# Local attention, first query tile: score products that move 128 columns instead of 256

## The chip, the cores and the metric

The kernel runs on one core of one Trainium2 chip. The metric is the device time of one execution in microseconds; the time before is the median of three runs, 640.8 us (640.77 to 642.25). The profile is one further execution, recorded instruction by instruction. Engines are named as the profile names them: PE (matrix products), PEld (the loading of a product's stationary operand, which overlaps PE), DVE (vector), ACT (activations), POOL, and SP, which issues DMAs.

## The reference

One transformer block on 512 tokens of width 1024, all in float32. A first half of the heads does a block-sparse attention with three branches; the second half does local attention ("swa") with a window of 128 tokens, and this is the part concerned here:

```python
def swa_attention(q, k, v, sinks, slopes):      # 8 heads, 2 key groups, 64 wide
    ...
    dist = C + i - j                             # C = 128
    valid = (dist >= 0) & (dist < SWA_WINDOW) & (kpos >= 0)
    s = jnp.einsum('bnqgrd,bnkgd->bngrqk', qb, kb).astype(jnp.float32) * scale
    s = s - slopes_g[:, :, None, None] * dist.astype(jnp.float32)
    s = jnp.where(valid[:, None, None], s, NEG_INF)
    m = jnp.maximum(jnp.max(s, axis=-1, keepdims=True), sg)
    e = jnp.exp(s - m)
    prob = e / (jnp.sum(e, axis=-1, keepdims=True) + jnp.exp(sg - m))
    o = jnp.einsum('bngrqk,bnkgd->bnqgrd', prob.astype(vb.dtype), vb)
```

Each tile of 128 queries sees its own 128 keys and the 128 before them. The first tile of queries has no keys before it, so its scores fill 128 columns and not 256. After attention come an output projection, a gated feed-forward part with a short convolution, and a gated per-layer embedding.

## The kernel before

Matrix products are made in a split form: each operand is a rounded high part and the rest as a low part, both of type float32r, so that a product is a sum of two or three float32r products. A query tile already holds its high and low parts stacked over the 128 partitions, so a score needs two: `score` (line 954) multiplies the same stationary query block with the high part of the keys (`kh`) and then with the low part (`kl`), into the same place in PSUM. Plain float32 products occur too, for short sums and for transposes: `rstd_col` (line 571) multiplies four blocks of a [128, 512] tile with a column of ones, one matmul call for each (lines 575 and 576); `compress_out` (line 858) makes one call for the keys (line 870) and two for the values (lines 871 and 872); `transpose_split` (line 892) transposes through PE with a 128x128 identity.

The attention runs in units: for the sparse half and then for the local half, for two key groups `g` each, the query tiles in the order 3, 0, 2, 1 (lines 1137 and 1138). A local unit is `swa_scores` (line 958). For `qt == 0` it sets `n = 128`, starts at key 0, and reads the second half of the table of distances (`b0 = P`). For each of four heads it makes the two products of `score` into half of a PSUM tile (two heads to a tile, three tiles of the tag "s" in rotation), and a fused DVE instruction that adds the scaled distances and takes the row's minimum with the sink (lines 971 to 979). Then ACT makes four exponentials with row sums, DVE takes reciprocals, and POOL scales the four rows. In the unit after, `pv` (line 922) transposes these probabilities on PE, ACT and DVE split the transposed tile into its two parts, and PE multiplies it with the values.

Between these steps `fill` (line 537) puts in work from other parts, which needs only PE and weights: the remaining query projections and the first part of the output projection (`out_proj_first`, line 1200). The functions lay out what is to be done with priorities and dependencies; the order of the instructions on the engines in the attention part is then made by the planner of the surrounding framework, which goes through the program with its own timing model (line 55). From `ple_load`, a little after the attention, to the end of the feed-forward part, the order is written out by the kernel itself and kept.

All eight units of the local half call `swa_scores`; those with `qt == 0` are the second of each key group. The line numbers in the profile are those of two helpers: L419 stands for everything in the attention part, so instructions are told apart there by the names of their tiles (`swa_pss` is the PSUM tile of the local scores).

Of the kernel before, what the change touches and what calls it, by code (L numbers as in the profile page):

```python
# [15 lines left out]
ALU = mybir.AluOpType  # L16
# [406 lines left out]
class Block:  # L423
# [534 lines left out]
    def swa_scores(self, u):  # L958
        self.phase = "swa"
        nc = self.nc  # L960
        g, qt = u["g"], u["qt"]
        kh, kl = self.ks
        n = P if qt == 0 else 2 * P
        k0 = 0 if qt == 0 else (qt - 1) * P
        b0 = P if qt == 0 else 0

        p = self.u([P, 4, 2 * P + 1], F32, "p")
        ns = self.nsink[:, 4 * g : 4 * g + 4]
        nc.gpsimd.tensor_copy(p[:, :, n], ns)
        nm = self.tiny([P, 4], "nm")  # L970
        for r in range(4):
            if r % 2 == 0:
                ps = self.ps("s")
            o = ps[:, r % 2 * 256 : r % 2 * 256 + 256]
            self.score(ps, o, self.q[4 + 2 * g + r // 2][:, r % 2, qt * P : (qt + 1) * P],
                       kh[:, g, k0 : k0 + 256], kl[:, g, k0 : k0 + 256])
            nc.vector.tensor_tensor_reduce(p[:, r, :n], o[:, :n], self.dist_w[:, b0:], op0=ALU.add, op1=ALU.min,
                                           scale=SLOPES[4 * g + r], scalar=ns[:, r : r + 1], accum_out=nm[:, r : r + 1])
            yield 100 if r < 3 else 4 * n + 380
        sm = self.tiny([P, 4], "sm")  # L980
        for r in range(4):
            nc.scalar.activation(p[:, r, : n + 1], p[:, r, : n + 1], AF.Exp, bias=nm[:, r : r + 1], scale=-1.0,
                                 accum_out=sm[:, r : r + 1])
        rc = self.tiny([P, 4], "rc")
        nc.vector.reciprocal(rc, sm)
        for r in range(4):
            self.scale_rows(p[:, r, :n], rc[:, r : r + 1])
        yield 400
        u["blocks"] = [
            ([p[:, r, b * P : (b + 1) * P] for r in range(4)], P,  # L990
             self.vs[k0 // P + b][:, 4 + g].rearrange("p a d -> p (a d)"))
            for b in range(n // P)
        ]
# [1128 lines left out]
```

## Time and profile before

| | |
|---|---|
| median of three runs | 640.8 us (640.77 to 642.25) |
| the profiled execution, its own time | 641.23 us |
| its span, from the first instruction to the last | 639.5 us |
| the local attention's scores, first to last | 153.9 to 195.9 us from the span's start |
| score products on PE (`swa_pss`) | 64, each of 256 columns |

The profile page gives busy times by engine, the span in 40 slices, the chain of work that ended last, and the costliest groups. The time of an answer is counted from the span's start. Two readings need care. A matmul's recorded duration is its latency through the array, and matmuls are pipelined: what one costs PE in a row of others is the spacing of their ends, not the recorded duration. And for the timeline, instructions of one kind that follow each other are merged into one row with the stretch from the first start to the last end and their number.

### The profile page before, as it was taken

The numbers are of one execution on the slowest core, as the hardware profiler recorded it, in microseconds if no ns is written. First come the engines' busy times: TensorE is split into PE (matmuls) and PEld (weight loads), VectorE is DVE, ScalarE is ACT, GpSimd is POOL, SyncE is SP. The second block draws the span as 40 slices with busy tenths as digits, with TensorE's granted clock in tenths as the row PEclk, the third lists the DMA queues.
The fourth block names the chain that finished last, engine by engine and source line by source line (L and its number), as shares of the span: only waits on it lengthen the run. The fifth ranks groups of instructions, "written<-read, shape, count | busy, mean of one in ns | idle before, by whom it ended". The sixth has DMA issues, their size and how long they took to land.

```text
span 639.5 us, 11315 instructions
## 1 busy us (share of the span) xinstructions
PE 633.3 (99%) x4071; PEld 575.6 (90%) x4071; DVE 511.1 (80%) x1029; ACT 396.3 (62%) x759; POOL 155.1 (24%) x240
## 2 busy tenths in 40 slices
PE   8999999999999999999999999999999999999997
PEld 7988888888888887888999999999998899999986
DVE  6796668978866498799898989989898985756973
ACT  7545579878898567474677777777754533343251
POOL 1001497787686100211001010102000010201000
PEclk9999999999999999999999999999999999999999
DMA  8416834221321658485465766687754534377032
GB/s 303 176 60 181 226 84 126 51 49 36 75 59 63 228 224 324 149 210 120 123 191 145 202 164 153 169 213 238 178 156 121 152 92 122 114 250 264 1 116 81
DMA packets 45288, 95.78 MB, mean 150 GB/s; under 512 B 4400, under 2 KB 13744, under 8 KB 44976
## 3 DMA queue, kind: packets, MB, share of 16 engines
q1 hardware_dynamic: 40208, 84.49, 40.8%
q0 software_dynamic: 4880, 10.49, 9.7%
q8 instruction: 32, 0.52, 0.3%
q14 instruction: 24, 0.20, 0.1%
q10 hardware_dynamic: 144, 0.08, 0.0%
HBM read 81.41 MB, written 9.44 MB: 142 GB/s over the span
## 4 chain that ended last, share of the span: by engine, by line
PE 97%; ACT 1%; DMA 1%; DVE 0%; issue 0%; SPq 0%; ACTq 0%
PE mlpup_psmm L201 23%; PE fill_psmm L419 10%; PE mlpup_pss L201 8%; PE mlpdown_pst L201 6%; PE mlpdown_pss L201 5%; PE mlpup_pst L201 5%; PE mlpdown_psmm L201 4%; PE nsa_pss L419 3%; PE nsa_pst L419 3%; PE nsa_pso L419 3%; PE norm_pss L201 3%; PE projq_psmm L419 3%; PE mlpup_pso L201 2%; PE vnatural_pss L419 2%; PE projk_psmm L419 2%; PE compress_psmm L419 2%
## 5 line engine op out<-in xcount | busy, mean ns | idle before, releaser
L201 PE MATMUL mlpup_psmm<-r_u,mlpup_wh 128*128 128x256 f32 (+1 forms) x612 | 79.4, 283 | 0.1
L201 PEld LDWEIGHTS mlpup_psmm<-r_u,mlpup_wh 128*128 128x128 f32 x612 | 76.0, 191 | 0.6 <-DVE mlpup_wh L201 0.4
L201 PE MATMUL mlpup_psmm<-mlpup_u,mlpup_wh 128*128 128x256 f32 (+1 forms) x474 | 69.6, 298 | 0.0
L201 PEld LDWEIGHTS mlpup_psmm<-mlpup_u,mlpup_wh 128*128 128x128 f32 x474 | 63.5, 190 | 2.6
L201 POOL DMA_DIRECT2D mlpup_u<-in_gs_dram x17 | 20.9, 1230 | 154.9 <-DVE mlpup_s L201 61.0
L201 ACT ACTIVATE mlpup_wh<-mlpup_u 128x1024 fp32r<-128x1024 f32 x37 | 39.2, 1060 | 25.2 <-PE mlpup_psmm L201 21.2
L201 ACT ACTIVATE mlpdown_wh<-mlpdown_wr 128x1024 fp32r<-128x1024 f32 (+1 forms) x24 | 23.7, 988 | 40.1 <-PE mlpdown_pst L201 10.7
L201 DVE TENSOR_TENSOR mlpup_wh<-mlpup_u,mlpup_wh 128x1024 fp32r<-128x1024 f32 x37 | 45.2, 1221 | 1.4 <-ACT mlpup_wh L201 0.5
L419 PE MATMUL fill_psmm<-loadx_u,fill_wh 128*128 128x512 f32 x144 | 45.2, 398 | 0.0
L201 PE MATMUL mlpdown_pst<-mlpup_u,mlpdown_wh 128*128 128x512 f32 (+1 forms) x228 | 45.0, 340 | 0.0
L201 PEld LDWEIGHTS mlpdown_pst<-mlpup_u,mlpdown_wh 128*128 128x128 f32 x228 | 37.0, 189 | 5.0
L201 DVE TENSOR_TENSOR mlpdown_wh<-mlpdown_wr,mlpdown_wh 128x1024 fp32r<-128x1024 f32 (+1 forms) x24 | 27.3, 1138 | 16.6 <-ACT mlpdown_wh L201 16.3
L419 POOL TENSOR_SCALAR nsa_u<-nsa_u,nsa_nrc,gate 128x512 f32<-128x512 f32 (+3 forms) x64 | 38.5, 619 | 5.4 <-DVE nsa_nrc L419 3.2
L419 ACT ACTIVATE nsa_u<-nsa_u,nsa_nnm 128x512 f32<-128x512 f32 (+3 forms) x64 | 35.2, 553 | 4.0 <-DVE nsa_nnm L419 3.7
L201 DVE TENSOR_TENSOR mlpup_wh<-mlpup_wr,mlpup_wh 128x1024 fp32r<-128x1024 f32 (+1 forms) x23 | 27.9, 1211 | 11.9 <-ACT mlpup_wh L201 11.9
L201 PE MATMUL mlpdown_pss<-mlpup_u,mlpdown_wh 128*128 128x256 f32 x246 | 35.9, 282 | 0.0
L201 POOL TENSOR_TENSOR mlpdown_s<-mlpdown_s,mlpdown_s 128x512 f32<-128x512 f32 x6 | 9.6, 1599 | 105.0 <-ACT mlpdown_s L201 104.8
L419 DVE TENSOR_TENSOR nsa_u<-nsa_pst,nsa_u 128x512 fp32r<-128x512 f32 (+1 forms) x43 | 28.9, 687 | 7.5 <-ACT nsa_u L419 7.2
L201 PEld LDWEIGHTS mlpdown_pss<-mlpup_u,mlpdown_wh 128*128 128x128 f32 x246 | 32.5, 191 | 0.3
L419 ACT ACTIVATE nsa_u<-nsa_pst 128x512 fp32r<-128x512 f32 x43 | 25.0, 596 | 12.0 <-PE nsa_pst L419 11.4
L419 DVE CUSTOM_DVE_ANT_0 nsa_u<-nsa_pss,biastables_u 128x128 f32<-128x128 f32 (+4 forms) x64 | 27.7, 449 | 4.8 <-PE nsa_pss L419 2.7
L201 PE MATMUL mlpdown_psmm<-mlpup_u,mlpdown_wh 128*128 128x256 f32 (+1 forms) x180 | 31.1, 320 | 0.0
(341 smaller groups left out, 1653.0 us busy)
## 6 DMA issues: line engine op xcount, KB each, us to landing
mlpup_u<-in_gs_dram SPq DMA_DIRECT2D x34, 512.0 KB, 5.5
mlpup_u<-in_gs_dram POOLq DMA_DIRECT2D x17, 512.0 KB, 7.0
mlpup_wr<-in_gs_dram SPq DMA_DIRECT2D x17, 256.0 KB, 4.1
fill_wr<-in_win_dram SPq DMA_DIRECT2D x6, 512.0 KB, 4.3
fill_u<-fill_u SPq DMA_DIRECT2D x20, 128.0 KB, 2.3
mlpdown_wr<-in_down_dram SPq DMA_DIRECT2D x5, 512.0 KB, 3.8
loadx_u<-in_xT_dram SPq DMA_DIRECT2D x8, 256.0 KB, 5.0
compress_u<-projk_u SPq DMA_DIRECT2D x16, 128.0 KB, 4.0
```

What stands on the lines that cost most here:

```text
L201: return f(*map(real, a), **{m: real(x) for m, x in k.items()})
L419: hold(x.call(*map(real, x.a), **{m: real(v) for m, v in x.k.items()}))
```

## The change

In the local units the two products of `score` get the `n` columns that are read, and not always 256. The offset of a head's scores in its PSUM tile stays (0 or 256). For `qt` of 1 to 3, `n` is 256 and nothing differs; for `qt == 0` the 16 products (two groups, four heads, two parts) move 128 columns of keys each. The columns dropped are keys 128 to 255, whose scores were written to PSUM and not read. The DVE instruction reads the same 128 columns as before.

```diff
             if r % 2 == 0:
                 ps = self.ps("s")
-            o = ps[:, r % 2 * 256 : r % 2 * 256 + 256]
+            o = ps[:, r % 2 * 256 : r % 2 * 256 + n]
             self.score(ps, o, self.q[4 + 2 * g + r // 2][:, r % 2, qt * P : (qt + 1) * P],
-                       kh[:, g, k0 : k0 + 256], kl[:, g, k0 : k0 + 256])
-            nc.vector.tensor_tensor_reduce(p[:, r, :n], o[:, :n], self.dist_w[:, b0:], op0=ALU.add, op1=ALU.min,
+                       kh[:, g, k0 : k0 + n], kl[:, g, k0 : k0 + n])
+            nc.vector.tensor_tensor_reduce(p[:, r, :n], o, self.dist_w[:, b0:], op0=ALU.add, op1=ALU.min,
                                            scale=SLOPES[4 * g + r], scalar=ns[:, r : r + 1], accum_out=nm[:, r : r + 1])
             yield 100 if r < 3 else 4 * n + 380
```

## The prediction

> **What bounds the kernel now.** I read the page first: the engines' busy shares, the granted clock and the chain of work that ended last.
>
> ```profile
> span 639.5 us, 11315 instructions
> PE 633.3 (99%) x4071; PEld 575.6 (90%) x4071; DVE 511.1 (80%) x1029; ACT 396.3 (62%) x759; POOL 155.1 (24%) x240
> PEclk9999999999999999999999999999999999999999
> PE 97%; ACT 1%; DMA 1%; DVE 0%; issue 0%; SPq 0%; ACTq 0%
> ```
>
> PE is busy for 633.3 of 639.5 us, at the full granted clock in every slice, and the chain that sets the end lies on PE for 97% of the span. So a nanosecond taken from PE in a stretch where the chain is on PE is a nanosecond of the end, and one added is one added. Next I looked at the stretch of the change, which holds the local scores, and at the stretch behind it up to the part whose order is fixed. The columns are the stretch, its length, and the busy time (with the number of instructions) of PE, PEld, DVE, ACT and POOL; then the granted clock.
>
> ```profile
> 150.00:200.00 50.00, 49.86 (x298) 42.85 (x297) 38.74 (x142) 45.71 (x131) 40.96 (x74) 1.00 0.24 65
> 200.00:240.00 40.00, 40.00 (x189) 33.10 (x188) 27.68 (x41) 25.55 (x42) 6.15 (x8) 1.00 0.54 193
> ```
>
> PE idles 0.14 us in 50, and not at all in the 40 after. Better order cannot bring more than those 0.14 us here; the rest of any gain must be shorter PE work. ACT is the second engine, 45.71 of 50 us.
>
> The third view is the tile of the local scores: its forms, and what waits for it. The last two rows are the view's "who waited for it".
>
> ```profile
> L419 PEld LDWEIGHTS swa_pss<-projq_u,fill_u x64: 187/188/192, 153.9 to 195.7; 128*128 128x128 f32 x64
> L419 PE MATMUL swa_pss<-projq_u,fill_u x64: 274/282/365, 154.1 to 195.9; 128*128 128x256 f32 x64
> L419 DVE CUSTOM_DVE_ANT_0 swa_u<-swa_pss,biastables_u,nsink x32: 320/476/484, 160.8 to 197.3; 128x256 f32<-128x256 f32 x24, 128x128 f32<-128x128 f32 x8
> ...
> who waited for it (us, times):
>   DVE swa_u L419: 2.1, 5
> ```
>
> All 64 products move 256 columns; 8 of the 32 DVE instructions that read them read 128, and these are the two units of the first query tile. Their 16 products are the ones that change.
>
> **The change part by part.** No instruction is added, removed or given a new wait; no DMA is touched. 16 products become half as wide; the DVE instruction reads the same 128 columns. The whole sum is 16 times the difference in the spacing of a product on PE. The chain of work has the first four of them as PE time, and the timeline shows rows of the same kind in an unbroken run, beside wider ones:
>
> ```profile
> 161.59 0.48 PE swa_pss L419 x4
> ...
> 190.98 0.64 PE L419 MATMUL swa_pss<-projq_u,fill_u 128*128 128x256 f32 x4
> ...
> 177.45 2.48 PE L419 MATMUL fill_psmm<-nsa_u,fill_wh 128*128 128x512 f32 x10
> ...
> L419 PE MATMUL fill_psmm<-nsa_u,fill_wh 128*128 128x512 f32 x10 | 2.5, 393 | 0.0
> ```
>
> In the chain four products take 0.48 us, 0.120 each. In the timeline, four take 0.64 from the first start to the last end; less one latency of 0.282 that is 0.36 for three, again 0.119. Ten of 512 columns take 2.48, less 0.393 that is 2.09 for nine, 0.232 each. So 256 more columns cost 0.113, or 0.44 ns a column, and 128 columns at that rate would take 0.120 - 0.056 = 0.064 us.
>
> But a product also loads its stationary operand, here 128x128. The narrowest products of the trace, one column against a loaded 128x128, show what remains when there is nothing to stream, and the transposes show it at 128 columns:
>
> ```profile
> 24.30 0.94 PE L419 MATMUL vnatural_pst<-ones,loadx_s 128*128 128x1 f32 x8
> ...
> L419 PE MATMUL vnatural_pst<-ones,loadx_s x8: 164/250/250, 24.3 to 25.0; 128*128 128x1 f32 x8
> ...
> 158.04 0.60 PE L419 MATMUL nsa_pst<-ident,nsa_u 128*128 128x128 f32 x4
> ...
> L419 PE MATMUL nsa_pst<-ident,nsa_u 128*128 128x128 f32 x144 | 23.0, 272 | 0.0
> ```
>
> Eight one-column products take 0.94, less the first's 0.164 that is 0.776 for seven: 0.111 each, with one column to move. Four transposes take 0.60, less 0.272 that is 0.33 for three: 0.109. So a product behind a fresh 128x128 load does not come closer than 0.11 to the one before it, whatever it moves. Both score products of a head load anew, though it is the same query block: the tile's view has 64 loads for 64 products.
>
> No float32r product in the trace moves fewer than 256 columns, so the cost at 128 is bounded from both sides:
>
> - From below 0.064 (the rate, if the load hid behind neighbours): 16 x (0.120 - 0.064) = 0.9 us less.
> - From above, two plain float32 products' worth: the first rival's rows show that one costs two loads and two passes, 2 x 0.111 = 0.222: 16 x (0.222 - 0.120) = 1.6 us more.
> - In between, the load: 16 x (0.120 - 0.111) = 0.14 us less.
>
> I take the load, 0.111. The nearest row by what an instruction carries is the float32r product of 256 columns: the type and the single load stay, only the columns halve; and the one-column rows say that the load then takes over as the limit. Against the profiled execution's own 641.23 us (span 639.5 plus 1.73 around it) the sum is 641.1; that execution is 0.43 above the median, so on the median it is 640.8 - 0.14 = 640.7 us. Moving one of the 16 off the chain would not alter this, since PE has no idle time to hide it in.
>
> What stays at nothing: DVE waits 2.1 us in five places for scores, and a score that is ready 0.01 us sooner moves that by as much; DVE is busy for 38.74 of 50 us and not on the chain. What could come besides is a new order: the planner lays the attention part out with a timing model, so products of another length can move their neighbours. I cost that at nothing as the likeliest, since PE has 0.14 us of idle time to win, and the fillers, which need no result of the unit, cover most short waits; its bad side is a rival.
>
> By the Trainium skill, "TensorE: Matmul & The Clock Gate", section "Back-to-back issue gap", a stream of loads and products of 128 columns sustains about 81 ns each; an estimate from that page would be 16 x (0.120 - 0.081), 0.6 us less. The same sentence gives about 131 ns for 512 columns, where the rows here give 232, so the trace does not agree.
>
> **The rivals.**
>
> *Below some width, float32r is worked like plain float32.* The trace shows that the plain form is dearer:
>
> ```profile
> 59.22 0.41 PE L419 MATMUL compressout_pss<-w,compressout_gv 128*31 128x64 f32 x4
> ...
> L419 PE MATMUL compressout_pss<-w,compressout_gv x4: 219/219/243, 59.2 to 59.4; 128*31 128x64 f32 x4
> ```
>
> The code calls two products there (lines 871, 872) and the trace has four; lines 575 and 576 call four and the trace has eight. So a plain product runs as two matmuls. And each streams slower: 0.41 less the first's 0.243 is 0.167 for three, 0.056 each for 64 columns, 0.87 ns a column against 0.44. At 128 columns each matmul then needs 0.111 by either limit, a product 0.222, and the sum is +1.6 us: 642.4. For it: nothing in the trace shows that narrow float32r keeps its rate. Against it: nothing shows a switch by width either, and if only the slower rate came and not the second matmul, 0.111 stays and so does my forecast.
> By the Trainium skill, "FP8 and Floating Point Precision", section "TensorE Precision Notes", true FP32 makes four passes through the array; the trace agrees, since two matmuls at half rate are four. An estimate from that rule is four times 128 columns, as long as the 512-column product: 1.8 us more.
>
> *A new order leaves PE waiting for ACT (the one that ends slower).* One place shows where:
>
> ```profile
> 172.71 1.09 ACT swa_u L419 x3
> 173.82 0.60 ACT swa_s L419
> 174.44 1.09 ACT swa_u L419 x3
> 175.54 1.14 PE swa_pso L419 x4
> ...
> L419 ACT ACTIVATE swa_u<-swa_u,swa_nm 128x257 f32<-128x257 f32 x24 | 12.0, 502 | 0.0
> L419 ACT ACTIVATION_READ_ACCUMULATOR swa_u<-swa_u,swa_nm 128x1 f32 x32 | 6.2, 193 | 0.0
> ```
>
> Between 172.71 and 175.54 the chain leaves PE for ACT, which evicts transposes between exponentials; PE idles 0.14 us there because other score products and transposes fill the rest. If the planner puts one unit's four exponentials ahead of such an eviction while PE has used up that filler, PE waits 4 x (0.502 + 0.193) = 2.8 us: 643.6. It decides as soon as the filler in front of the wait is over 0.14 us short; past 1.9 us of waiting the time is over 0.3% slower. For it: ACT at 91% of the stretch. Against it: no wait of PE on ACT appears elsewhere in it.
>
> *The load hides, and the products run at 0.064.* Then 640.8 - 0.9 = 639.9. Against it are the one-column rows at 0.111. Even if all 16 products cost nothing, that would be 1.9 us, so the mechanism has no way to more than 0.3%.
>
> **How the numbers follow.** About 0.3% (1.9 us, so 638.9 to 642.7) is what a measurement of this kernel can tell from no change. Chances: load-bound at 640.7, 0.50; the same with an order that costs or gives a few tenths, 0.09; worked as plain float32 at 642.4, 0.26, of which a third falls above the bound with a little waiting on top; new order with PE waiting, 643.6, 0.12; load hidden, 639.9, 0.03. Faster by over 0.3% is left at 0.03 for what I do not see. Slower: 0.12 + 0.08 = 0.20; same 0.77. The range 639.6 to 643.0 takes in both bounds of the unknown product (639.9 and 642.4), and leaves out most of the waiting case.
>
> **What would show each step right or wrong.** Right: 16 `swa_pss` products of 128 columns, four in a row spaced by about 0.11, PE busy to within some tenths of all 90 us from 150 to 240. The plain-float32 rival shows as 0.22 a product, or as 80 instead of 64 `swa_pss` matmuls. The load-hidden rival shows as 0.06. The order rival shows as idle time of PE in 150 to 200 above 0.14, released by ACT. I would be wrong altogether if time moved outside this stretch, or if the order of the parts after the attention changed.

## The result and the profile after

The changed kernel takes 646.0 us (median of 20 runs, 642.18 to 650.61), the kernel before 641.0 (20 runs, 640.24 to 644.83): a ratio of 1.0066, 95% interval 1.0046 to 1.0085 (the medians alone give 1.0078). It is slower, by 0.66%, and its times spread over 8 us instead of 5.

The profiled execution is the shortest of the 20, 642.18 us, so the first profile shows little of the loss. The rows of its page that answer to those of before:

```profile
span 640.5 us, 11306 instructions
PE 633.8 (99%) x4071; PEld 575.5 (90%) x4071; DVE 512.8 (80%) x1029; ACT 396.5 (62%) x759; POOL 156.6 (24%) x240
PE 97%; DVE 2%; ACT 0%; issue 0%; DVEq 0%
```

The chain of work still lies on PE for 97%, but 2% of it is now on DVE, where before it had 0%. The table by stretches (columns as in the prediction; the last two are the DMA engines' busy share and GB/s):

```profile
28.00:50.00 22.00, 21.26 (x117) 17.88 (x116) 21.54 (x40) 11.94 (x19) 3.48 (x5) 1.00 0.32 111
62.00:80.00 18.00, 17.96 (x86) 14.69 (x86) 10.48 (x38) 9.13 (x19) 6.48 (x6) 1.00 0.81 210
150.00:200.00 50.00, 50.00 (x295) 43.10 (x293) 36.77 (x128) 42.02 (x118) 35.32 (x65) 1.00 0.37 101
200.00:240.00 40.00, 40.00 (x189) 33.02 (x188) 28.38 (x42) 27.00 (x48) 10.35 (x12) 1.00 0.53 181
```

From 150 to 240 us, where the change was made, PE is fully busy; it idles for 0.74 us from 28 to 50 us instead, where before's table of PE alone has it busy throughout:

```profile
28.00:50.00 22.00, 22.00 (x124) 1.00 0.34 128
```

The view of PE's waits (what waited for what: us in total, times, longest) has two there, both for DVE, that before does not have:

```profile
PE projk_psmm L419 <- DVE projk_wh L419: 0.6, 1, 0.6
PE compress_pss L419 <- DVE compress_wh L419: 0.2, 1, 0.2
```

The tile's view of the local scores:

```profile
L419 PE MATMUL swa_pss<-projq_u,fill_u x64: 220/280/363, 154.6 to 197.4; 128*128 128x256 f32 x48, 128*128 128x128 f32 x16
```

and, from the timeline of PE, the longest run of the changed products:

```profile
168.10 0.89 PE L419 MATMUL swa_pss<-projq_u,fill_u 128*128 128x128 f32 x7
```

There are 64 score products as before, 16 of them of 128 columns. The seven in a row have start times in the trace that lie 0.060 us apart once, behind a wider product, and then 0.110 to 0.114. Over all 16, the next product starts 0.058 to 0.062 us later in the five places where a wider product stands ahead, and 0.110 to 0.114 us later in the other 11.

The order of the instructions differs from before's on all five engines, and long ahead of the first product that changed (161.4 us in before): on DVE and POOL within the first 2 us, on ACT from 28, on SP from 38 and on PE from 47 us on. The planner's own loop (its last call shortened, a comment added) says how that can be:

```python
for _ in range(PASSES):                      # PASSES = 6
    done, end = self.schedule(live, begin)
    if best is None or end < best[0]:
        best = end, done
    self.dues(done, begin, live)
for x in best[1]:
    hold(x.call(...))
```

It makes six candidate orders of the whole attention part. The first goes by program order alone, each later one by due times taken from the one ahead; the one with the lowest modelled end is played. By the planner's own microseconds before plays its fourth candidate (231.79). With 16 products shorter, the modelled ends fall out otherwise, and the changed kernel plays its first (232.67): an order that was never refined, and 0.88 worse by the planner's own reckoning than what before plays.

The planner stands in the kernel's own file (the loop is lines 413 to 420), not in a framework around it, and line 263 is its price of a float32r product of n columns, in us:

```python
return max(.058, .009 + .000431 * n)
```

That gives 0.119 for 256 columns, as measured, and 0.064 for 128, where the changed kernel's products in a row show 0.110 to 0.114. With 0.111 as the least price, the same loop has the changed kernel's fourth candidate lowest again, at 231.65. This was worked through off the chip, and no run plays it, but by it the choice was tipped by a price that the chip does not give.

### The profile page after: what moved, and what is told of

It reads as the page before. It is cut to its first block, busy times and chain, and to the rows that moved or that the text cites. A ratio compares the mean times of both kernels' runs of the same rounds, so it can differ in the third digit from the quotient of the medians.

```text
span 640.5 us, 11306 instructions
## 1 busy us (share of the span) xinstructions
PE 633.8 (99%) x4071; PEld 575.5 (90%) x4071; DVE 512.8 (80%) x1029; ACT 396.5 (62%) x759; POOL 156.6 (24%) x240
## 4 chain that ended last, share of the span: by engine, by line
PE 97%; DVE 2%; ACT 0%; issue 0%; DVEq 0%
PE mlpup_psmm L201 23%; PE fill_psmm L419 10%; PE mlpup_pss L201 8%; PE mlpdown_pst L201 6%; PE mlpup_pst L201 5%; PE mlpdown_pss L201 5%; PE mlpdown_psmm L201 4%; PE nsa_pss L419 3%; PE nsa_pst L419 3%; PE nsa_pso L419 3%; PE norm_pss L201 3%; PE projq_psmm L419 3%; PE mlpup_pso L201 2%; PE vnatural_pss L419 2%; PE projk_psmm L419 2%; PE swa_pso L419 1%
## 5 line engine op out<-in xcount | busy, mean ns | idle before, releaser
L201 PE MATMUL mlpup_psmm<-mlpup_u,mlpup_wh 128*128 128x256 f32 (+1 forms) x474 | 69.4, 297 | 0.0
L419 POOL TENSOR_TENSOR fill_wh<-fill_wr,fill_wh 128x1024 fp32r<-128x1024 f32 (+2 forms) x13 | 24.5, 1887 | 38.8 <-DVE compress_u L419 22.2
```

The costliest lines, as they stand in the source:

```text
L201: return f(*map(real, a), **{m: real(x) for m, x in k.items()})
L419: hold(x.call(*map(real, x.a), **{m: real(v) for m, v in x.k.items()}))
```

## The experiments

**Products or order.** Two kernels separate the two things that the change did. Both resize the 16 products in the finished program, after the order has been made, so that each order meets each width. Each has one of the two lines (the comments are added, and the function that they call is left out):

```diff
     with tile.TileContext(nc, **TCARGS) as tc:
         build(tc, io)
+    resize(nc, 128)      # planned at 256; the 16 products narrowed: old_order_128
+    resize(nc, 256)      # planned at 128; the 16 products widened: new_order_256
```

Expected of the first:

> The order of before is kept for every engine; only the 16 products are narrowed to 128 columns, in the finished program. If the products themselves cost the time (theory A, dearer narrow float32r), this is slower than before by what the change is, some 5 us (646). If the time comes from the new order of the whole program (theory B), it is at before or 0.1 to 0.2 us below it, 640.8 to 641.0, with 128-column products 0.111 us apart and little spread between executions.

and of the second:

> The order of the changed kernel is kept for every engine; only the 16 products are widened back to 256 columns in the finished program, so the arithmetic is that of before. Theory A: back at before, 641. Theory B: as slow as the changed kernel, a median of about 646, with the same wide spread (642 to 651), PE waiting near 36 us for the split weights of the first key projection.

Measured in five rounds: old_order_128 640.88 us, ratio 0.9993 (0.9985 to 1.0002); new_order_256 645.44 us, ratio 1.0063 (1.0041 to 1.0085). With the new order the time is the changed kernel's although no product is shorter, and with the old order it cannot be told from before's although all 16 are. The two traces have before's and the changed kernel's order on every engine. The loss belongs to the order.

Since before and old_order_128 have one order on PE, their timelines also show what the 16 products give. The first rows here are before's, from the first of the 16 to the first instruction behind the wider products that follow the last; the second are old_order_128's:

```profile
161.43 0.65 PE L419 MATMUL swa_pss<-projq_u,fill_u 128*128 128x256 f32 x4
188.46 1.03 PE L419 MATMUL swa_pst<-ident,swa_u 128*128 128x128 f32 x8
...
160.68 0.56 PE L419 MATMUL swa_pss<-projq_u,fill_u 128*128 128x128 f32 x4
187.58 1.04 PE L419 MATMUL swa_pst<-ident,swa_u 128*128 128x128 f32 x8
```

From start to start that is 27.03 us and 26.90: 0.13 less.

**An order that differs only in the local attention.** With 160 columns the planner's order leaves before's, its fourth candidate, only within the second local unit: in the traces no engine's order differs ahead of 163.9 us.

```diff
-            o = ps[:, r % 2 * 256 : r % 2 * 256 + 256]
+            w = 160 if qt == 0 else 256; o = ps[:, r % 2 * 256 : r % 2 * 256 + w]
             self.score(ps, o, self.q[4 + 2 * g + r // 2][:, r % 2, qt * P : (qt + 1) * P],
-                       kh[:, g, k0 : k0 + 256], kl[:, g, k0 : k0 + 256])
+                       kh[:, g, k0 : k0 + w], kl[:, g, k0 : k0 + w])
```

> The 16 products move 160 columns, and the planner orders the program anew; its order then differs from that of before only from the second local unit on (about 161 us), not in the first 160 us. If the slowdown comes from the early part of the new order (B1), this is at before, 640.8 to 641.5. If any new order in the local attention costs it (B2, the rival of the prediction: PE waits for ACT there), this is slower too, by 2 us or more.

Measured: 641.91 us, ratio 1.0013 (1.0001 to 1.0025): 0.4 us above the range of B1, and far below B2's. In its profile PE is busy for all 90 us from 150 to 240. A new order there costs a tenth of a per cent or two, not the loss.

**A second profile of the changed kernel**, without an edit, since the first was its shortest execution.

> The changed kernel once more, for a second profile: its 20 executions spread from 642.2 to 650.6, and the one profiled was the shortest. Theory B1: a longer execution shows longer waits of PE between 27 and 60 us, or a lower granted clock behind such a wait, and the same 64 products as before at 0.111.

It took 645.68 us, span 644.0. Between 27 and 60 us, where longer waits were expected, there are the same two of 0.6 and 0.2 us. New in its view of PE's waits is:

```profile
PE nsa_pss L419 <- DMA compress_u<-projk_u: 2.3, 1, 2.3
```

PE in stretches of 2 us around it (stretch, length, busy time with instructions, granted clock, DMA share, GB/s):

```profile
72.00:74.00 2.00, 2.00 (x12) 1.00 1.04 286
74.00:76.00 2.00, 0.13 (x1) 1.00 1.06 248
76.00:78.00 2.00, 1.53 (x8) 0.98 0.92 328
78.00:80.00 2.00, 2.00 (x7) 0.50 0.98 232
80.00:82.00 2.00, 2.00 (x9) 0.67 0.60 132
82.00:84.00 2.00, 2.00 (x14) 1.00 0.96 251
```

Beside the two early waits there is a third, of 2.3 us at 74 us, which neither the first profile nor before's has: the sparse attention's first scores (`nsa_pss`) wait for their key rows (`compress_u`). And behind it the clock is halved for some 3 us: 2 us at 0.50 and 2 at 0.67 give the work of 2 x 0.50 + 2 x 0.67 = 2.3 us in 4, so 1.7 us more are lost. Wait and clock together, 4.0 us, are about the 3.5 by which this span is longer than the first profile's; with the two early waits, 0.8 us, they are about the 4.5 by which it is longer than before's. new_order_256 has the same wait at 3.2 us, and its table by stretches shows the clock down for longer:

```profile
76.00:78.00 2.00, 0.97 (x2) 0.51 0.68 171
78.00:80.00 2.00, 2.00 (x7) 0.50 0.88 258
80.00:82.00 2.00, 2.00 (x7) 0.50 0.94 202
82.00:84.00 2.00, 2.00 (x10) 0.78 0.87 184
```

The chain of work of the same profile, followed back from that wait, names the cause (start, length, what; the short pieces and most of SP's are left out):

```profile
48.77 1.23 DVE projq_wh L419
...
50.07 6.09 DMA projq_wr<-in_win_dram
...
56.25 0.04 ACT projq_wh L419
...
57.99 1.13 DVE projq_wh L419
59.13 0.61 DVE projq_u L419
...
59.76 0.46 SPq L419
...
61.39 4.02 DMA projq_u<-projq_u
...
65.52 0.64 ACT projq_u L419
...
66.19 0.70 DVE projq_u L419
...
72.42 3.92 DMA compress_u<-projk_u
...
76.47 0.94 PE nsa_pss L419 x4
```

A weight (`projq_wr`) is loaded when DVE has freed a raw buffer, at 50.07 us; it takes 6.09 us to land. ACT and DVE split it into its parts, and behind that split in their queues stands the split of the first query projection (`projq_u`), which does not need the weight. On SP's queue a filler's load that needs this weight's raw buffer stands ahead of the query's last two moves. So all of them wait for the weight: the query's moves, the next splits that need the buffers these moves read, and in the end the key rows. The changed kernel's two profiles, one program in one order, bear this out: the load is issued at 50.06 and 50.07 us, ACT's split of it starts at 54.97 in the first and 56.25 in the second, the key rows' eight moves are issued from 67.90 and from 69.33 on, and PE waits for them for under 0.1 us and for 2.3.

In before, DVE's queue has the two splits the other way round. Before's timeline of DVE:

```profile
55.74 0.68 DVE L419 TENSOR_TENSOR projq_u<-projq_s,projq_u 128x512 fp32r<-128x512 f32 x1
56.34 1.22 DVE L419 TENSOR_TENSOR projq_wh<-projq_wr,projq_wh 128x1024 fp32r<-128x1024 f32 x1
```

and that of the changed kernel's second profile:

```profile
57.91 1.22 DVE L419 TENSOR_TENSOR projq_wh<-projq_wr,projq_wh 128x1024 fp32r<-128x1024 f32 x1
59.04 0.69 DVE L419 TENSOR_TENSOR projq_u<-projq_s,projq_u 128x512 fp32r<-128x512 f32 x1
```

**Which candidate is played.** In each kernel one candidate is forced, by its number. Each has one of the two added lines (with the comments added here).

```diff
-            if best is None or end < best[0]:
+            if _ == 3:      # changed kernel: narrow_pass4
+            if _ == 0:      # kernel before: wide_pass1
                 best = end, done
```

> The planner makes six candidate orders and plays the one whose modelled end is lowest. Modelled ends (the planner's own microseconds): with 256 columns 233.61, 232.66, 231.91, 231.79, 232.64, 232.64, so the fourth is played; with 128 columns 232.67, 233.90, 233.43, 232.86, 233.72, 233.72, so the first is played, the one that goes by program order alone. This kernel is the changed one, products and planning at 128 columns, but plays its fourth candidate; that one has before's order on every engine up to the second local unit, at about 161 us. Theory A (the time is lost because another candidate is played, early in the kernel): 640.5 to 641.9, ratio 0.998 to 1.002, no wait of PE of over 1 us for the key rows at 76 us. Rival B (planning at 128 columns costs the time, whichever candidate is played, through the order of the local attention): 644 to 646, ratio over 1.004.

> The kernel before, products and planning at 256 columns, but it plays its first candidate (modelled end 233.61 against 231.79 for the fourth). Up to the local attention its order is that of the changed kernel. Theory A (the first candidate's early order costs the time, and no product does): 644.5 to 646.5, ratio 1.005 to 1.009, with DVE's late low part of the key weight at about 36 us and a wait of PE for the key rows at about 76 us in the longer executions. Rival B (the loss needs the 128-column planning): 640.5 to 642, ratio within 0.998 to 1.002.

wide_pass1 took 644.43 us, ratio 1.0058 (1.0046 to 1.007), as theory A had it: before's own products, planned at their own width, are slow in the first candidate's order (its range in ratios held, and in us it began at 644.5). narrow_pass4 took 642.49 us, ratio 1.0024 (1.0013 to 1.0035): most of the loss is gone, but not all; theory A's range for it (up to 641.9) was missed. From 20 us on, PE has these waits in wide_pass1:

```profile
PE nsa_pss L419 <- DMA compress_u<-projk_u: 1.8, 1, 1.8
PE projk_psmm L419 <- DVE projk_wh L419: 0.6, 1, 0.6
PE compress_pss L419 <- DVE compress_wh L419: 0.2, 1, 0.2
```

and these in narrow_pass4:

```profile
PE swa_pso L419 <- ACT swa_u L419: 0.5, 1, 0.5
PE r_pst L201 <- DVE outproj_s L419: 0.2, 1, 0.2
```

The first set is the changed kernel's. The second is one wait in the local attention, for ACT, and one behind it, for DVE. The first of these is the prediction's own rival, at 0.5 us instead of 2.8.

**Where in the first candidate's order.** Four kernels play the changed kernel's order with a few instructions moved, and all else on every engine as it was. Each forces the first candidate and hands it to a function `reorder`; shown are the lines of that function that do the moving, where `named(x, s)` asks whether the tile that x writes has a name that starts with s. In the first, ten instructions of the gates (two on ACT, eight on DVE), which stand from about 28 us on in the changed kernel, go behind DVE's second weight split, at about 49.

```diff
-            if best is None or end < best[0]:
+            if _ == 0:
...
-        for x in best[1]:
+        for x in reorder(best[1]):
...
+    gate = [x for x in order if x.engine in ("ACT", "DVE") and any(v.tile.kw.get("tag") == "ge" for v in x.writes + x.reads)][2:]
+    last = [x for x in order if x.engine == "DVE" and x.writes[0].tile.kw.get("name", "").startswith("projq_wh")][1]
+    order = [x for x in order if x not in gate]
+    k = order.index(last) + 1
+    return order[:k] + gate + order[k:]
```

> The changed kernel's order with ten instructions moved: two ACT exponentials and eight DVE instructions of the gates (busy 28.4 to 31.9 us in the changed kernel, some 1.64 us of DVE's time) go behind DVE's second low part of a first-projection weight; every other instruction on every engine stays in its place. Reckoned from the trace of the second profile of the changed kernel: the key weight's low part on DVE goes from 35.86 to about 34.2 us, PE's 0.6 us wait for it goes; DVE's second low part goes from 48.77 to about 47.3 (ACT's high part of it ends there), so the load of the third first-projection weight is issued at about 48.6 instead of 50.06 (48.84 in the kernel before). Theory A1 (DVE's late work frees the raw buffer late, the load lands late, and the key rows of the sparse attention come late by that): 641 to 643, PE's wait of 2 to 3 us at 76 us gone or under 1 us, granted clock 1.0. Rival A2 (the load's place is not what decides; the rows are late because of the order of the DMA issues and of ACT and DVE from 56 us on): 644.5 to 646, the wait at 76 us still there.

Measured: 644.79 us, ratio 1.0058 (1.0039 to 1.0076), and one wait of PE from 20 us on:

```profile
PE nsa_pss L419 <- DMA compress_u<-projk_u: 1.0, 1, 1.0
```

Its chain of work has the load:

```profile
49.66 4.72 DMA projq_wr<-in_win_dram
```

The two early waits went, and the time hardly moved: it is in the range of rival A2. The load was issued at 49.66 us, not at the 48.6 that I had reckoned, and PE, 0.8 us earlier now, only reaches the late key rows sooner. Theory A1 falls in the form it was given: a moment set by a chain off PE swallows what PE gains ahead of it. (The profile is the shortest of the kernel's six executions, 642.69 us.)

The second moves the first query's split ahead of the late weight's on ACT and DVE, and its last moves ahead of the load on SP.

```diff
+    s = next(x for x in order if x.engine == "DVE" and named(x, "projq_s"))
+    q = [x for x in order if x is not s and any(v.tile is s.writes[0].tile for v in x.reads)]
+    wh = [x for x in order if x.engine == "ACT" and named(x, "projq_wh")][2]
+    t = q[0].writes[0].tile
+    moves = [x for x in order if x.engine == "SP" and any(v.tile is t for v in x.reads)]
+    fill = next(x for x in order[order.index(moves[0]):] if x.engine == "SP" and named(x, "fill_wr"))
...
+    order = [x for x in order if x not in q and x is not wh]
+    k = order.index(s) + 1
+    order = order[:k] + q + [wh] + order[k:]
+    order.remove(fill)
+    order.insert(order.index(moves[3]) + 1, fill)
```

> The changed kernel's order with four instructions and one load moved: the high and low part of the first query projection (one instruction on ACT, one on DVE) go ahead of the split of the late weight, and that projection's last two key-row-sized moves on SP's queue go ahead of the load that waits for that weight's raw buffer. Nothing else moves; PE's and POOL's order are unchanged. Theory C (the in-order queues carry the late weight's landing on to PE: ACT's and DVE's split of it stands ahead of the query's split, and SP's next load stands ahead of the query's moves, so everything behind it, the key rows of the sparse attention too, is late by it): ACT's query split goes from 57.4 to about 55.3 us and DVE's from 59.0 to about 56, the query's last moves from 60.9 to under 59, the second query's moves from 66.2 to about 62, the key rows land by some 74.6; PE's wait of 1.8 to 3.2 us at about 74 us goes to under 0.6, the clock stays 1.0, and only the 0.8 us of early waits are left: 641.2 to 642.8, ratio 1.000 to 1.003. Rival D (the rows are late because their own transfers are slow on a wire that is 80% busy from 62 to 80 us, whatever the queues' order): the wait stays at 1 to 3 us, 644 to 646.

The third makes both moves:

> Both moves together: the ten gate instructions behind DVE's second low part as in gates_late, and the first query's split and moves ahead as in query_first. By theory C, no wait of PE between 28 and 80 us of over 0.6 us is left and the clock stays 1.0: 640.4 to 642.0, ratio 0.998 to 1.002, so that the whole loss is accounted for by two places of the order. Rival D: 643.5 to 645.5, as gates_late.

query_first took 642.24 us, ratio 1.0022 (1.0008 to 1.0036); query_and_gates 641.17 us, ratio 1.0002 (0.9992 to 1.0011). From query_first's timelines of DVE and SP:

```profile
55.65 0.69 DVE L419 TENSOR_TENSOR projq_u<-projq_s,projq_u 128x512 fp32r<-128x512 f32 x1 [0.70 <-ACT projq_u L419]
57.34 1.22 DVE L419 TENSOR_TENSOR projq_wh<-projq_wr,projq_wh 128x1024 fp32r<-128x1024 f32 x1
...
66.02 4.98 SPq L419 DMA_DIRECT2D compress_u<-projk_u  x8
```

and PE from 62 to 80 us, in its table by stretches (columns as above):

```profile
62.00:80.00 18.00, 18.00 (x90) 1.00 0.85 211
```

DVE's query split is at 55.65 us instead of 59.04, and the key rows are issued from 66.02 on (67.90 and 69.33 in the two profiles of the changed kernel). The wait at 74 us is gone and the clock full, while the DMA share of the stretch, 0.85, is as high as it was (0.81 and 0.82). This profile is the shortest of 12 executions, and the changed kernel's shortest has almost none of that wait either, so it is the median that decides: at 642.24 us, under the 644 to 646 of rival D, D falls. Three of the 12 executions took 644.4 to 645.6 us; none of these was profiled, and the wait may still come in them. What stays in its view of PE's waits are the two early ones, of 0.6 and 0.2 us. With the gates moved as well these go too; the same table of query_and_gates:

```profile
28.00:50.00 22.00, 21.86 (x122) 1.00 0.37 139
62.00:80.00 18.00, 18.00 (x90) 1.00 0.78 204
```

PE idles 0.14 us in these 40 us. So twelve instructions on ACT and DVE and two DMA issues, put elsewhere in the changed kernel's order, give back what the change cost.

The fourth tries another reading of SP's queue: in the new order the second group's key rows are issued ahead of the first group's, which are read first.

```diff
+    rows = [x for x in order if x.engine == "SP" and x.writes[0].tile.kw.get("tag") == "kn"]
+    late, first = rows[4:8], rows[8:12]
+    order = [x for x in order if x not in late]
+    k = order.index(first[-1]) + 1
+    order = order[:k] + late + order[k:]
+    return order
```

> The changed kernel's order with four DMA issues moved on SP's queue: the four moves of the second group's key rows, which the sparse attention reads only after its first group, go behind the four moves of the first group's. Theory C: the first group's rows are not ready before about 71.2 and 72 us (ACT's and DVE's split of the key projection, late by the chain ahead of them), so the last of the four is issued at about 73.7 instead of 74.3: the wait shrinks by 0.6 to 1.1 us, from about 2.3 to 1.2 to 1.7, and the time by about as much, 643.5 to 645.5. Rival E (the place of the second group's moves on the queue is the cause): 2.5 us of issues go from ahead of the rows, the wait goes altogether, 641.3 to 642.8.

Measured: 646.65 us, ratio 1.0088 (1.0062 to 1.0114), above what either theory gave. From its view of PE's waits:

```profile
PE nsa_pss L419 <- DVE nsa_nmp L419: 2.0, 1, 2.0
PE nsa_pss L419 <- DMA compress_u<-projk_u: 1.3, 1, 1.3
```

and from SP's timeline:

```profile
68.86 0.53 SPq L419 DMA_DIRECT2D fill_wr<-in_win_dram  x1
71.34 5.95 SPq L419 DMA_DIRECT2D compress_u<-projk_u  x8
```

The wait for the first group's rows shrinks to 1.3 us, as theory C had it, since SP now stands idle from 69.4 to 71.34 until they are made; rival E falls. Of what is behind on SP's queue, the next load is issued at 77.34 us, 3 us later than in the second profile of the changed kernel, and a wait of 2.0 us comes up later, which I had not counted: by the chain of work, the second group's rows land at 79.07, ACT's next query split starts behind them, and eight exponentials that PE needs stand behind that split until 82.64.

## Why the prediction was wrong

It gave 640.7 us, a range of 639.6 to 643.0 and 0.20 for slower by over 0.3%; the time is 646.0.

- **What bounds the kernel** was right: PE, and each idle moment of PE is one of the end. Every loss above is a wait of PE, or the clock behind one.
- **The term of the products** came out right: 0.13 us less between the same instructions of before and old_order_128, for 0.14 forecast. That is too little for any interval here; old_order_128's (0.9985 to 1.0002) allows it. The reason given holds in 11 of the 16 places, where the spacing of 0.110 to 0.114 us is the load's 0.111, not 0.064 and not 0.222; there are 64 `swa_pss` matmuls and not 80. So the rival with plain float32 falls. "Whatever it moves" was too strong: in the five places behind a wider product the spacing is 0.058 to 0.062, as the hidden-load rival had it. It gains little, since a wider product behind takes most of it back: the two 512-column products behind the first four take 0.47 us in before (161.91 to 162.38) and 0.52 in old_order_128 (161.07 to 161.59). By the Trainium skill, "TensorE: Matmul & The Clock Gate", section "Back-to-back issue gap", a stream of 128-column pairs runs at about 81 ns; the 0.110 to 0.114 us of these float32r products in a row do not agree.
- **The step that failed** is "What could come besides is a new order ... I cost that at nothing as the likeliest, since PE has 0.14 us of idle time to win, and the fillers ... cover most short waits". The 0.14 us bounds what a better order can win, and says nothing of what a worse one can lose. And it was read from 150 to 200 us only, as if the planner would re-lay just the units with other products. It lays the whole attention part out anew, chooses among six candidates, and the change tipped that choice. In place of nothing the new order alone costs 0.63% (new_order_256): in the second profile 3.1 us of waits of PE and 1.7 us of lowered clock.
- **The rival with a new order** had the right sign and the wrong place. It was put at ACT in the local attention, at 2.8 us. There the profiles show at most 0.5 us of it (narrow_pass4). The loss came from 28 to 84 us, ahead of all local attention: DVE late with two weight splits, and a weight's landing handed on through ACT's, DVE's and SP's queues to the key rows.
- **"I would be wrong altogether if time moved outside this stretch"**: it did.
- **The chances**, a slip beside the argument: the five that are named add up to 1.00 without the 0.03 for faster, so these 0.03 were taken from "same" without a word.

What stays open: why narrow_pass4 lies 0.24% above before. Its profile has two waits of PE, together 0.7 us, against 1.4 us in the medians; the rest was not looked for with a run. Nor is it known why the one load lands earlier in some executions than in others. None of the versions beats the kernel before by more than the measurement can tell; the fastest is old_order_128.

## What to carry to other kernels

Where a planner makes the order, a shorter instruction is two changes: itself, and a new order of all that is planned with it. Before pricing the first, check the planner's price for the new length against a trace, lay the new order beside the old one, and see from which instruction they differ; afterwards separate the two by giving each order both widths. In an in-order queue, look at what stands behind an instruction that waits for a DMA: a load with no slack hands its landing time, and the spread of it, on to everything behind it.

## What the runs showed of the hardware

- A wait of PE of 2.3 us was followed by half the granted clock for 3.4 us, and so was one of 2.0 us (keys_first, 4.3 us behind another of 1.3). One of 3.2 us brought 6.8 us of it, the first 1.0 still within the wait. Behind one of 1.8 us (wide_pass1) and one of 1.0 (gates_late) it stayed at 1.00 in every 2 us up to 92. So each of these waits of 2.0 us and more cost PE about three quarters as much again, or more. By the Trainium skill, "TensorE: Matmul & The Clock Gate", section "What's actually happening", the clock falls after an idle window of about 3.4 us; the 2.3 us here are shorter than that, and the clock fell all the same.
- The clock's own records in these traces say when. In all three it falls a whole number of times 3.413 us after it first went full: 21 times in the second profile of the changed kernel and in new_order_256, 23 times in keys_first. Count time in such steps of 3.413 us: in the step ahead of each fall PE idled 1.97, 2.25 and 1.97 us, and the waits without a fall put 1.77 (wide_pass1), 1.3 (the first of keys_first) and 0.97 us (gates_late) into one step. So the idle time within one step fits all six waits; where between 1.77 and 1.97 us the limit lies, and whether it is the same in another kernel, no run here shows.
- The same weight's load took 6.09 us to land in the second profile of the changed kernel and 4.72 in gates_late's chain. In an order without slack that difference reaches PE. In the profiles with the changed kernel's early order, the load took 5.77 us in wide_pass1, 6.09 in the second profile and 6.26 in new_order_256, and PE waited 1.8, 2.3 and 3.2 us for the key rows; in the first profile, where ACT's split starts 4.91 us after the issue, under 0.1. The spread of the changed kernel's times, 642.18 to 650.61 us, is most likely this, though no run varied the landing by itself.
